# Gated linear attention: queries multiplied at half width and copied into the padded tile by GpSimd; one more block size written by ScalarE

## The chip, the cores and the metric

One core of one Trainium2 chip. Times are microseconds of device time from the start to the end of one execution on that core. A time of a kernel is the median of several executions. The engines are TensorE (PE in the profile), VectorE (DVE), ScalarE (ACT), GpSimd (POOL) and SyncE (SP), which here only issues DMAs.

## The reference

One layer of a decoder trunk, 2048 tokens and 16 learned meta tokens, width 1024, float32. Half of the mixer's heads are gated linear attention (GLA), half attention over a sliding window with a sink; a feed-forward part with a squared ReLU follows.

```
h = h + concat(o_gla, o_swa) @ w_out        # both from rmsnorm(h) @ w_in
h = h + relu(rmsnorm(h) @ w1)^2 @ w2
```

The change is in the GLA half, which the reference writes as a scan over chunks of 64 tokens:

```
b = cumsum(g, axis=2)                                   # log decays, per channel
decay = exp(where(causal, b_i - b_j, -inf))
A = einsum('bhid,bhjd,bhijd->bhij', q, k, decay)
o = einsum('bhij,bhjv->bhiv', A, v) + einsum('bhid,bhdv->bhiv', q * exp(b), S)
S = exp(b_last) * S + einsum('bhjd,bhjv->bhdv', k * exp(b_last - b), v)
```

There are 4 heads of 64 query channels and 128 value channels.

## The kernel before

**The square of scores.** The decay between tokens i and j is a product over the channels, so A is no plain product of q and k. The kernel builds it by levels. `gla_pair` handles 256 tokens (two blocks of 128) at a time, so it runs eight times, as pairs 1 to 8. It holds q and k as `qk` (128 partitions are the channels of two heads; two such head pairs; 256 tokens). For each block size s = 1, 2, 4, 8, 16, 32, 64, `gla_level` multiplies the queries of every odd block of s tokens with the keys of the even block before it (matmuls into the PSUM tile `lv`, L1304), and writes these s x s squares to their places in `AT`, 128 by 128 per head. Then it multiplies the even blocks' keys (L1310) and the odd blocks' queries (L1312) by the level's decay factors from `decays`, so that the next level, with blocks twice as large, finds both relative to the new block borders. Small squares lie on many places of the tile and are written by VectorE through a mask (`copy_predicated`, L1322); for s = 32 and 64 ScalarE copies them (L1315).

**The padded queries.** Two heads share the 128 partitions of a matmul's contraction. To keep them apart, the queries stand in `qpad`, a tile of 128 partitions by 2 heads by 2 head pairs by 256 tokens: head 0 has its values in partitions 0 to 63 and zeros in 64 to 127, head 1 the other way round. The zeros are written once. There is one `qpad` for the whole kernel. At the start of a pair GpSimd copies the queries into it (L1343, L1344), and from then on L1312 multiplies in it, over zeros and values alike: twice as many elements as q has. At the end of a pair `gla_out` multiplies `qpad` with the state S (L1409) and `AT` with v (L1408).

**What runs beside it.** The kernel is mostly dense products in split float32 on TensorE: each weight tile is loaded (`raw`), rounded by ScalarE to a high part (`wh`, L139), and VectorE takes the remainder as the low part (`wl`, L141); three matmuls per tile use them (L178, L179, L180). The tiles `raw`, `wh` and `wl` have three buffers each, and some low parts are stored to DRAM (`lows`) and loaded again later. The GLA pairs run next to the input projection's second half and the feed-forward parts, together with the sliding-window attention: for each block of 128 tokens scores `sc` (L1031, L1032, in two PSUM buffers), a masked copy to `p` with its maximum on VectorE (L1033, with `sst`), exponentials on ScalarE (L1041), the scaling of `p` by GpSimd (L1056), transposes `tr` (L1076) split into `ph` and `pl`, with masks by GpSimd (L1091), the part of the meta tokens (`trm`, `pm` L1065, `ptm` L1068 by GpSimd), `pv`, and outputs `oT` stored to `mix` (by GpSimd's DMA queue at L1114, by SyncE's at L1113).

**What sets the order.** The program is written as Python generators. `drive` (L2230) steps a generator of dense work, and at each of its pauses `mix_stage` (L2237) steps the streams `gla` and `swa` once. The framework then schedules the recorded instructions onto the queues of the engines; on each engine they run in that queue's order, and wait on semaphores for each other. So an edit of one instruction can move others.

Of the kernel before, what the change touches and what calls it, by code (L numbers as in the profile page):

```python
# [13 lines left out]
ALU = mybir.AluOpType  # L14
# [3 lines left out]
P = 128  # L18
# [28 lines left out]
class Layer:  # L47
# [1244 lines left out]
        nc.vector.tensor_copy(eB, factor[P].rearrange("p (a j) -> p a j", a=2))  # L1292
        yield factor, eB

    def gla_level(self, s, qpad, k, AT, factor):

        nc = self.nc
        li = LEVELS.index(s)
        ps = self.gpsum("lv")
        for j in range(2):  # L1300
            for hp in range(2):
                ql = qpad[:, :, hp, j * P : (j + 1) * P].rearrange("p h (n two s) -> p h n two s", two=2, s=s)
                at = (2 * j + hp) * P
                nc.tensor.matmul(  # L1304
                    ps[:, at : at + P], lhsT=k[:, hp, j * P : (j + 1) * P], rhs=ql[:, :, :, 1, :], start=True, stop=True
                )
        n = 256 // s
        f = factor[s].rearrange("p (n two) -> p n two", two=2)
        kv = k.rearrange("p a (n two s) -> p (a n) two s", two=2, s=s)[:, :, 0, :]
        nc.vector.tensor_tensor(kv, kv, f[:, :, 1:2].to_broadcast([P, n, s]), ALU.mult)  # L1310
        qv = qpad.rearrange("p h a (n two s) -> p h (a n) two s", two=2, s=s)[:, :, :, 1, :]
        nc.vector.tensor_tensor(qv, qv, f[:, :, 0:1].unsqueeze(1).to_broadcast([P, 2, n, s]), ALU.mult)  # L1312
        if s >= 32:
            for r in range(0, P, 2 * s):
                nc.scalar.activation(  # L1315
                    AT[r : r + s, :, r + s : r + 2 * s],
                    ps.rearrange("p (h n) -> p h n", h=8)[r : r + s, :, r // 2 : r // 2 + s], AF.Copy,
                )
            return
        av = AT.rearrange("p h (n two s) -> p h n two s", two=2, s=s)  # L1320
        mk = self.lmask[:, li, :].rearrange("p (n s) -> p n s", s=s)
        nc.vector.copy_predicated(  # L1322
            av[:, :, :, 1, :], mk.unsqueeze(1).to_broadcast([P, 8, 64 // s, s]),
            ps.rearrange("p (h n s) -> p h n s", h=8, s=s),
        )

    def gla_pair(self, c, gp, now, outs, state, more):
        nc = self.nc
        qk, gates = now
        qpad, q, k = self.qpad, qk[:, 0:2, :], qk[:, 2:4, :]  # L1330

        next(outs, None)
        yield
        next(outs, None)
        factor, eB = next(gates)
        yield
        next(outs, None)
        next(state, None)
        AT = gp.tile([P, 8, P], F32, name="AT", tag="AT", bufs=1)
        qkp = AT.rearrange("p h n -> p (h n)")[:, :512].rearrange("p (a n) -> p a n", a=2)  # L1340
        nc.vector.tensor_tensor(qkp, q, k, ALU.mult)
        nc.vector.tensor_tensor(q, q, factor[1].rearrange("p (a n) -> p a n", a=2), ALU.mult)
        nc.gpsimd.tensor_copy(qpad[0:64, 0], q[0:64])  # L1343
        nc.gpsimd.tensor_copy(qpad[64:P, 1], q[64:P])  # L1344
        yield
        next(outs, None)
        next(state, None)
        ps = self.pd.tile([P, NB], F32, name="dg", tag="d")
        for j in range(2):
            for hp in range(2):  # L1350
                nc.tensor.matmul(
                    ps[:, 4 * j + 2 * hp : 4 * j + 2 * hp + 2], lhsT=qkp[:, hp, j * P : (j + 1) * P], rhs=self.hsel,
                    start=True, stop=True,
                )
        dg = gp.tile([P, 8], F32, name="dg", tag="dg")
        nc.vector.tensor_copy(dg, ps[:, 0:8])
        for h in range(4):
            nc.scalar.activation(AT[:, h, :], self.ident, AF.Copy, scale=dg[:, h : h + 1])
        yield
        next(outs, None)  # L1360
        for h in range(4, 8):
            nc.scalar.activation(AT[:, h, :], self.ident, AF.Copy, scale=dg[:, h : h + 1])
        v = self.gla_values(c, gp)
        for s in reversed(LEVELS):
            self.gla_level(s, qpad, k, AT, factor)
            yield
            next(outs, None)
            next(state, None)
            if s == LEVELS[1] and more:
                gates = self.gla_front(gp, self.gla_gates(c + 1, gp))  # L1370
                next(gates)
            if s == LEVELS[0]:
                ps = self.pd.tile([P, NB], F32, name="kT", tag="d")
                for j in range(2):
                    for hp in range(2):
                        nc.tensor.transpose(
                            ps[:, (2 * j + hp) * P : (2 * j + hp + 1) * P], k[:, hp, j * P : (j + 1) * P], self.ident
                        )
                kT = gp.tile([P, 4 * P], F32, name="kT", tag="kT")
                nc.scalar.activation(kT, ps, AF.Copy)  # L1380
                if more:
                    next(gates)
                    self.next = self.gla_keys(c + 1, gp), gates
            else:
                yield

        def outs():
            parts = [
                self.gla_out(2 * c + j, gp, AT[:, 4 * j : 4 * j + 4, :], qpad[:, :, :, j * P : (j + 1) * P],
                             kT[:, 256 * j : 256 * j + 256], v[:, j, :], eB[:, :, j : j + 1])  # L1390
                for j in range(2)
            ]
            next(parts[0])
            yield
            yield from parts[0]
            next(parts[1])
            yield
            yield from parts[1]

        return outs()  # L1400
# [1232 lines left out]
```

## Time and profile before

| | |
|---|---|
| median of 3 runs | 2072.09 us (2071.88 to 2073.42) |
| the profiled execution | 2071.57 us, of which its span is 2069.9 |
| mean clock granted to TensorE | 0.998 |
| instructions in the span | 28255 |
| the eight pairs' levels | 243 to 800 us |

How to read the profile's rows: an engine's row gives its busy time, its share of the span and its instructions. A row of a group gives line, engine, operation, output<-inputs, shapes and count, then busy time and mean, then the idle time just before. A row of the timeline gives the start, the duration, the engine, the line and the operation; in brackets stands how long the engine idled before it and what ended that. A row of TensorE's waits gives the matmul that waited, what it waited for, the total, the number and the longest. Ends of matmuls are modelled, and neighbours on an engine overlap a little.

### The profile page before, as it was taken

To read this page: it belongs to the slowest core of one execution; us is meant where nothing else is said; L and a number is where in the kernel's file an instruction comes from. 1 tells how busy PE (TensorE), PEld (TensorE's weight loads), DVE (VectorE), ACT (ScalarE), POOL (GpSimd) and SP (SyncE) were. 2 spreads that over 40 slices of the span, in tenths; PEclk is the share of its full clock that TensorE was granted. 3 is DMA by queue.
4 is the path that set the end of the run, shared out by engine and by line. 5 is a ranking of instruction groups with operands and counts; after the bars stand their busy time and mean duration, and the time that the engine had idled before them with its cause. 6 is when DMAs were issued, how large, how long until landed. Compare 5 with 4: busy or idle time off the path is not lost.

```text
span 2069.9 us, 28255 instructions
## 1 busy us (share of the span) xinstructions
PE 2046.7 (99%) x9995; PEld 1727.0 (83%) x9995; DVE 1572.1 (76%) x2641; ACT 1057.7 (51%) x1975; POOL 223.3 (11%) x378
## 2 busy tenths in 40 slices
PE   9999999999999999999999999999999999999998
PEld 7988799888888888788888888888888888888887
DVE  7867867987998887776666867777766775785876
ACT  7524556565677576554444333443545545333434
POOL 0000134333434332000000000000000000000000
PEclk9999999999999999999999999999999999999999
DMA  7436534556766777935448753496355458654412
GB/s 262 153 121 212 175 90 111 154 151 194 221 188 191 254 241 241 342 108 168 147 143 279 268 191 103 169 326 216 133 177 178 151 180 311 255 191 133 153 50 82
DMA packets 190366, 383.58 MB, mean 185 GB/s; under 512 B 18320, under 2 KB 73872, under 8 KB 190224
## 3 DMA queue, kind: packets, MB, share of 16 engines
q1 hardware_dynamic: 182064, 377.85, 53.8%
q0 software_dynamic: 8160, 3.93, 1.9%
q8 instruction: 78, 1.28, 0.3%
q14 instruction: 64, 0.52, 0.1%
HBM read 260.67 MB, written 120.98 MB: 184 GB/s over the span
## 4 chain that ended last, share of the span: by engine, by line
PE 87%; DVE 7%; DMA 3%; ACT 2%; issue 1%; SPq 0%; POOL 0%; DVEq 0%; ACTq 0%; POOLq 0%
PE psq L179 9%; PE psq L180 9%; PE psq L178 9%; PE psw L179 8%; PE psw L178 8%; PE psw L180 8%; PE psd L179 7%; PE psd L178 7%; PE psd L180 7%; PE psv L653 2%; PE lv L1304 2%; DMA x<-x 1%; PE psd L460 1%; PE psd L461 1%; PE psd L459 1%
## 5 line engine op out<-in xcount | busy, mean ns | idle before, releaser
L180 PE MATMUL psw<-bl,wh 128*128 128x512 f32 x728 | 283.2, 389 | 0.0
L178 PE MATMUL psw<-bh,wh 128*128 128x512 f32 x728 | 283.2, 389 | 0.0
L179 PE MATMUL psw<-bh,wl 128*128 128x512 f32 x728 | 283.2, 389 | 0.0
L178 PE MATMUL psq<-oh,wh 128*128 128x512 f32 x672 | 262.2, 390 | 0.0
L180 PE MATMUL psq<-ol,wh 128*128 128x512 f32 x672 | 261.4, 389 | 0.0
L179 PE MATMUL psq<-oh,wl 128*128 128x512 f32 x672 | 261.4, 389 | 0.0
L1604 ACT ACTIVATE wh<-rw 128x1024 fp32r<-128x1024 f32 x91 | 96.5, 1061 | 276.9 <-PE psw L180 242.1
L1605 DVE TENSOR_TENSOR wl<-rw,wh 128x1024 fp32r<-128x1024 f32 x91 | 111.3, 1223 | 111.0 <-ACT wh L1604 111.0
L178 PEld LDWEIGHTS psw<-bh,wh 128*128 128x128 f32 x728 | 136.6, 188 | 28.6
L180 PEld LDWEIGHTS psw<-bl,wh 128*128 128x128 f32 x728 | 136.6, 188 | 28.5
L179 PEld LDWEIGHTS psw<-bh,wl 128*128 128x128 f32 x728 | 136.6, 188 | 28.0
L178 PEld LDWEIGHTS psq<-oh,wh 128*128 128x128 f32 x672 | 126.1, 188 | 26.8 <-issue 0.5
L179 PEld LDWEIGHTS psq<-oh,wl 128*128 128x128 f32 x672 | 126.1, 188 | 26.6 <-issue 0.5
L180 PEld LDWEIGHTS psq<-ol,wh 128*128 128x128 f32 x672 | 126.1, 188 | 26.1
L178 PE MATMUL psd<-u,wh 128*128 128x512 f32 x320 | 129.6, 406 | 1.8 <-DVE st L279 1.1
L179 PE MATMUL psd<-u,wl 128*128 128x512 f32 x320 | 125.8, 393 | 0.1
L180 PE MATMUL psd<-u,wh 128*128 128x512 f32 x320 | 125.7, 393 | 0.0
L1604 ACT ACTIVATE wh<-r 128x1024 fp32r<-128x1024 f32 x56 | 59.3, 1060 | 114.0 <-PE psq L180 107.0
L2498 DVE TENSOR_TENSOR bl<-b,bh 128x1024 fp32r<-128x1024 f32 x91 | 110.8, 1218 | 0.2
L139 ACT ACTIVATE wh<-raw 128x1024 fp32r<-128x1024 f32 (+2 forms) x70 | 73.0, 1044 | 68.1 <-PE psd L180 46.2
L178 PE MATMUL psd<-m,wh 128*128 128x512 f32 x256 | 101.7, 397 | 0.0
L179 PE MATMUL psd<-m,wl 128*128 128x512 f32 x256 | 100.0, 391 | 0.4 <-DVE wl L1751 0.4
(438 smaller groups left out, 4959.7 us busy)
## 6 DMA issues: line engine op xcount, KB each, us to landing
r<-w SPq DMA_DIRECT2D x56, 512.0 KB
rw<-w2q SPq DMA_DIRECT2D x52, 512.0 KB
b<-hops SPq DMA_DIRECT2D x49, 512.0 KB
b<-hops_j SPq DMA_DIRECT2D x42, 512.0 KB
wl<-lows SPq DMA_DIRECT2D x39, 512.0 KB
raw<-w SPq DMA_DIRECT2D x36, 512.0 KB
raw<-wo SPq DMA_DIRECT2D x32, 512.0 KB
lows<-wl SPq DMA_DIRECT2D x28, 512.0 KB
```

Source lines behind the costliest of these rows:

```text
L139: nc.scalar.activation(wh, raw, AF.Copy)
L178: nc.tensor.matmul(ps, lhsT=wh, rhs=ah, start=first, stop=False, skip_group_check=skip)
L179: nc.tensor.matmul(ps, lhsT=wl, rhs=ah, start=False, stop=False, skip_group_check=skip)
L180: nc.tensor.matmul(ps, lhsT=wh, rhs=al, start=False, stop=last, skip_group_check=skip)
L459: nc.tensor.matmul(ps, lhsT=ah, rhs=wh, start=kt == 0, stop=False)
L460: nc.tensor.matmul(ps, lhsT=ah, rhs=wl, start=False, stop=False)
L461: nc.tensor.matmul(ps, lhsT=al, rhs=wh, start=False, stop=kt == KT - 1)
L653: nc.tensor.matmul(ps, lhsT=x, rhs=y[:, w], start=new and i == 0 and k == 0 and n == 0, stop=i == 1 and k == 1 and n == 2, skip_group_chec ...
L1304: nc.tensor.matmul(ps[:, at : at + P], lhsT=k[:, hp, j * P : (j + 1) * P], rhs=ql[:, :, :, 1, :], start=True, stop=True)
L1604: nc.scalar.activation(wh, src, AF.Copy)
L1605: return (wh, wl), lambda: nc.vector.tensor_tensor(wl, src, wh.bitcast(F32), ALU.subtract)
L2498: self.nc.vector.tensor_tensor(l, self.B[s], h.bitcast(F32), ALU.subtract)
```

## The change

`gla_level` gets `q`, the half of `qk` that holds the queries, beside `qpad`. It multiplies the odd blocks in `q`, 128x256 elements without the zeros, and GpSimd copies the multiplied blocks into `qpad`, with one copy per head on 64 partitions: two copies per level, 112 in all. And the squares of block size 16 go to `AT` by ScalarE, with four copies of 16 partitions, where VectorE's masked copy wrote them; L1322 runs 32 times instead of 40. The copies at a pair's start are now written as a loop and are the same instructions. Behind the edit the lines of the file move by four or five (L1322 is L1326, L1469 is L1474).

```diff
-    def gla_level(self, s, qpad, k, AT, factor):
+    def gla_level(self, s, qpad, q, k, AT, factor):
...
         nc.vector.tensor_tensor(kv, kv, f[:, :, 1:2].to_broadcast([P, n, s]), ALU.mult)
-        qv = qpad.rearrange("p h a (n two s) -> p h (a n) two s", two=2, s=s)[:, :, :, 1, :]
-        nc.vector.tensor_tensor(qv, qv, f[:, :, 0:1].unsqueeze(1).to_broadcast([P, 2, n, s]), ALU.mult)
-        if s >= 32:
+        qv = q.rearrange("p a (n two s) -> p (a n) two s", two=2, s=s)[:, :, 1, :]
+        nc.vector.tensor_tensor(qv, qv, f[:, :, 0:1].to_broadcast([P, n, s]), ALU.mult)
+        for h in range(2):
+            r = slice(64 * h, 64 * h + 64)
+            pv = qpad[r, h].rearrange("p a (n two s) -> p (a n) two s", two=2, s=s)[:, :, 1, :]
+            nc.gpsimd.tensor_copy(pv, qv[r])
+        if s >= 16:
             for r in range(0, P, 2 * s):
                 nc.scalar.activation(
...
-        nc.gpsimd.tensor_copy(qpad[0:64, 0], q[0:64])
-        nc.gpsimd.tensor_copy(qpad[64:P, 1], q[64:P])
+        for h in range(2):
+            r = slice(64 * h, 64 * h + 64)
+            nc.gpsimd.tensor_copy(qpad[r, h], q[r])
...
-            self.gla_level(s, qpad, k, AT, factor)
+            self.gla_level(s, qpad, q, k, AT, factor)
```

The instructions are scheduled anew, and some stand elsewhere. Three places follow, the rows of one engine each: line, operation, output<-inputs, shape, count. The first is GpSimd in pair 8, over the last levels, before:

```order
L1056 TENSOR_SCALAR p<-p,sst 128x128 x4
L1114 DMA mix<-oT 64x4x128
L1056 TENSOR_SCALAR p<-p,sst 128x128 x4
L1068 TENSOR_SCALAR ptm<-pm_1849,vecs 128x128 x4
L1091 AFFINE_SELECT ph<-ph 128x512
L1091 AFFINE_SELECT pl<-pl 128x512
```

And of the change:

```order
L1056 TENSOR_SCALAR p<-p,sst 128x128 x4
L1316 COPY qpad<-qk 64x16x16 x2
L1056 TENSOR_SCALAR p<-p,sst 128x128 x4
L1316 COPY qpad<-qk 64x8x32 x2
L1114 DMA mix<-oT 64x4x128
L1068 TENSOR_SCALAR ptm<-pm_1849,vecs 128x128 x4
L1316 COPY qpad<-qk 64x4x64 x2
L1091 AFFINE_SELECT ph<-ph 128x512
L1091 AFFINE_SELECT pl<-pl 128x512
```

The copies of a level stand behind the attention's steps of four `p` scalings, and ahead of the next such step; the store of `mix` moved behind two of them.

The second place is VectorE in pair 7, around block sizes 4 and 8, with the numbers of the tiles. The three `wl` there are the low parts of three weights that follow each other. Before:

```order
L1312 TENSOR_TENSOR qpad_1851<-qpad_1851,decays_7012 128x128x4
L1322 COPY_PREDICATED AT_7264<-lmask_320,lv_7561 128x128x4
L1469 TENSOR_TENSOR m_7636<-mx_7631,m_7636 128x512
L141 TENSOR_TENSOR wl_7658<-raw_7655,wh_7657 128x1024
L1033 ISA p_7608,sst_7609<-sc_7610,tabs_316 128x272
L1033 ISA sst_7609 128x1
L1033 ISA p_7608,sst_7609<-sc_7614,tabs_316 128x272
L1033 ISA sst_7609 128x1
L141 TENSOR_TENSOR wl_7738<-raw_7735,wh_7737 128x1024
L1065 TENSOR_TENSOR pm4_1849<-trm_7600,pm4_1849 64x128
L1558 TENSOR_TENSOR h_5967<-h_5967,psd_7576 128x512
```

And of the change:

```order
L1326 COPY_PREDICATED AT_7366<-lmask_320,lv_7667 128x128x4
L1312 TENSOR_TENSOR qk_7215<-qk_7215,decays_7112 128x32x8
L141 TENSOR_TENSOR wl_7768<-raw_7765,wh_7767 128x1024
L141 TENSOR_TENSOR wl_7853<-raw_7850,wh_7852 128x1024
L1065 TENSOR_TENSOR pm4_1849<-trm_7708,pm4_1849 64x128
L1033 ISA p_7716,sst_7717<-sc_7718,tabs_316 128x272
L1033 ISA sst_7717 128x1
L1033 ISA p_7716,sst_7717<-sc_7722,tabs_316 128x272
L1033 ISA sst_7717 128x1
L1563 TENSOR_TENSOR h_6043<-h_6043,psd_7684 128x512
```

The two reads of scores (L1033) moved behind the second `wl` and behind `pm`; the multiply of the queries for block size 8 stands ahead of the first `wl`, one level earlier than before.

The third place is VectorE in pair 6, ahead of and around block size 2. Before, the low part `wl_6714` of a weight of `w1` stands among the end of the previous pair's work:

```order
L912 TENSOR_TENSOR kr_1846<-ft_6281,kr_1846 64x128
L1422 TENSOR_TENSOR o_6421<-o_6412,gst_6422 128x512
L1052 TENSOR_TENSOR p_6285<-p_6285,sst_6286 128x64
L141 TENSOR_TENSOR wl_6714<-raw_6711,wh_6713 128x1024
L1432 TENSOR_TENSOR S_1850<-S_1850,kv_6493 64x256
L92 SCALAR_TENSOR_TENSOR nt_6481<-psn_6477,ny_6480 128x512
```

In the change the low part of the same weight is `wl_6803`:

```order
L1310 TENSOR_TENSOR qk_6341<-qk_6341,decays_6238 128x128x2
L1326 COPY_PREDICATED AT_6520<-lmask_320,lv_6738 128x256x2
L920 TENSOR_TENSOR vc_6784<-vr_6368,vc_6784 128x2x64
L920 TENSOR_TENSOR vd_6788<-vr_5974,vd_6788 128x2x64
L141 TENSOR_TENSOR wl_6803<-raw_6800,wh_6802 128x1024
L1538 SCALAR_TENSOR_TENSOR fr_6760<-psd_6725,rb_6564 128x512
L1312 TENSOR_TENSOR qk_6341<-qk_6341,decays_6238 128x64x4
L141 TENSOR_TENSOR wl_6880<-raw_6877,wh_6879 128x1024
```

It moved by some 30 rows, to behind the masked copy of block size 2 and the two steps `vc` and `vd` that prepare values for the attention. TensorE's products with it, `psd`, stand where they stood, and so does nearly every other matmul.

## The prediction

> **What bounds the kernel now.** I read the page's busy times and its chain first, then the table of windows, then TensorE's waits.
>
> ```profile
> PE 2046.7 (99%) x9995; PEld 1727.0 (83%) x9995; DVE 1572.1 (76%) x2641; ACT 1057.7 (51%) x1975; POOL 223.3 (11%) x378
> ...
> PE 87%; DVE 7%; DMA 3%; ACT 2%; issue 1%; SPq 0%; POOL 0%; DVEq 0%; ACTq 0%; POOLq 0%
> ```
>
> TensorE is busy 99% of the span and holds 87% of the chain that ended last. An edit to VectorE, ScalarE and GpSimd can pay only through TensorE's idle time. Where is that, in the stretch that the change touches? The edited levels run from 243 to 800 us; the next rows are two of eight windows, one per pair of chunks, the sum of the eight, and a window behind the levels (from:to, length, then busy time with its count per engine, granted clock, DMA share, GB/s).
>
> ```profile
> 311.00:380.00 69.00, 66.09 (x440) 62.08 (x439) 55.73 (x149) 44.09 (x128) 28.22 (x46) 1.00 0.50 140
> ...
> 673.00:747.00 74.00, 71.52 (x394) 61.08 (x393) 62.77 (x159) 48.51 (x131) 27.24 (x46) 1.00 0.81 260
> ...
> sum 550.00, PE 542.91 PEld 473.60 DVE 464.09 ACT 351.68 POOL 210.66; mean PE 67.86 PEld 59.20 DVE 58.01 ACT 43.96 POOL 26.33
> ...
> 900.00:1000.00 100.00, 100.00 (x441) 82.45 (x440) 72.09 (x96) 50.80 (x73) 0.00 (x0) 1.00 0.44 146
> ```
>
> In those 550 us TensorE idles 550.00 - 542.91 = 7.1 us; from 900 us on there is nothing left to win. VectorE idles 86 us there, so it is loaded but not full. What ended the long waits of TensorE (total, times, longest):
>
> ```profile
> PE psd L459 <- ACT st L466: 2.0, 1, 2.0
> PE psd L179 <- DVE wl L141: 1.4, 1, 1.4
> PE sc L1031 <- DVE sst L1033: 1.3, 2, 1.1
> ...
> PE tr L1076 <- POOL p L1056: 0.6, 1, 0.6
> ```
>
> The 2.0 us on ScalarE lie in the second pair (317.6 us). So VectorE and GpSimd cause at most 7.1 - 2.0 = **5.1 us**, the most the change can win. No row has TensorE waiting for `qpad` or `lv`: what the change speeds up is never waited for now.
>
> **The change, part by part.** Per-line durations (min/median/max in ns):
>
> ```profile
> L1310 DVE TENSOR_TENSOR qk<-qk,decays x56: 392/424/858, 245.3 to 794.8; 128x256 f32<-128x256 f32 x56
> L1312 DVE TENSOR_TENSOR qpad<-qpad,decays x56: 676/684/1130, 245.6 to 795.6; 128x512 f32<-128x512 f32 x56
> L1322 DVE COPY_PREDICATED AT<-lmask,lv x40: 686/720/1330, 246.2 to 781.9; 128x512 f32<-128x512 uint8 x40
> L1315 ACT ACTIVATE AT<-lv 32x256 f32<-32x256 f32 x16 | 5.9, 368 | 0.5 <-PE lv L1304 0.4
> L1343 POOL COPY qpad<-qk x8: 602/604/1505, 221.9 to 741.4; 64x512 f32<-64x512 f32 x8
> L1056 POOL TENSOR_SCALAR p<-p,sst x128: 361/370/1961, 241.4 to 790.6; 128x128 f32<-128x128 f32 x128
> ```
>
> *VectorE.* 56 multiplies of 128x512 become 56 of 128x256, the shape of L1310: 56 x (684 - 424) = 14.6 us less. Eight copies of L1322 go, at 0.72 each 5.8 us. That is 20 us less in 464, on an engine that is off the chain for most of this stretch. Alone it is worth only what it takes from the 5.1 us.
>
> *ScalarE.* Block size 16 needs four activations per pair, 32 in all. They are smaller (16 partitions by 128 elements) than the 32x256 row at 0.368; I take 0.31 to 0.37, 10 to 12 us more. ScalarE has 198 of the 550 us free. Its result `AT` is first read at the pair's end, so I cost it at nothing; if ScalarE were late by a whole group of four, 1.5 us of casts behind it would be late, still ahead of most readers.
>
> *GpSimd.* 112 copies of 64x256 are new, and no row has this shape. A line through 128 elements at 0.361 and 512 at 0.602 gives about 0.44 (an estimate from rows of two operations), so 0.9 us for the two of a level and 49 us in all. Bounds: 0.36 each (the 128-element row) and 1.5 each (the longest 512-element copy, made beside VectorE work): 0.7 to 3.0 us per pair. The likeliest is 0.9, since both rows are mostly at their minimum. GpSimd goes from 211 to 260 of 550 us.
>
> *The new wait.* The next level's `lv` product used to wait for a VectorE multiply; now it also waits for two GpSimd copies, which stand in GpSimd's queue behind softmax scaling (`p`, `ptm`), masks and `mix` stores. Behind the copies, in turn, wait those operations and TensorE's transposes of `p`. For each of the 48 gaps between two levels of a pair I took the end of the GpSimd work ahead of the copies plus 0.9 us against the start of the next `lv`. Most leave 2 to 6 us. Six leave under 1 us; the tightest and one more:
>
> ```profile
> 424.84 2.70 POOL L1056 TENSOR_SCALAR p<-p,sst 128x128 f32<-128x128 f32 x4
> 428.26 1.05 PE L1304 MATMUL lv<-qpad,qk 128*128 128x128 f32 x8
> ...
> 789.46 2.31 POOL L1056 TENSOR_SCALAR p<-p,sst 128x128 f32<-128x128 f32 x4
> ...
> 793.17 1.05 PE L1304 MATMUL lv<-qpad,qk 128*128 128x128 f32 x8
> ```
>
> At 424.84 + 2.70 + 0.9 = 428.44 the copies are done, 0.2 after the product's start; at 789.46 + 2.31 + 0.9 = 792.67 they are 0.5 before it. The other four leave 0.4, 0.6, 0.9 and 1.0. With the estimate the six cost 0.2 us, with half a microsecond of stretch at each 0.8; the work ahead of the copies may stretch too, so **+1.0** (0 to +2.5).
>
> *Order, pair 7 (the first moved place).* The reads of the first score pair (L1033) stood between two low-part products `wl`; now they stand behind both and behind `pm`.
>
> ```profile
> 697.88 0.43 DVE L1033 CUSTOM_DVE_ANT_0 p<-sc,tabs 128x272 f32<-128x272 f32 x1
> ...
> 699.26 1.23 DVE L141 TENSOR_TENSOR wl<-raw,wh 128x1024 fp32r<-128x1024 f32 x1 [0.59 <-ACT wh L139]
> 700.52 0.29 DVE L1065 TENSOR_TENSOR pm<-trm,pm 64x128 fp32r<-64x128 f32 x1
> ...
> 698.52 0.37 PE L1031 MATMUL sc<-kr,qs 128*128 128x272 f32 x1
> ...
> 703.51 0.39 PE L1031 MATMUL sc<-kr,qs 128*128 128x272 f32 x1 [1.06 <-DVE sst L1033]
> ```
>
> The second `wl` waits for ScalarE's `wh`, hence for a weight's DMA, and can't come earlier. So the first read starts at 700.52 + 0.29 = 700.8 and ends at 701.2. The next scores, due at 698.52, need its PSUM buffer (there are two): a new wait of 2.7. In return the third pair's reads are earlier against TensorE, and the 1.06 at 703.51 goes: **+1.6** (0 to +2.7; 0 if the pair's earlier relief lets the weight's DMA start sooner).
>
> *Order, pair 6 (the second).* A `w1` weight's low part, made at 595.52, now stands behind `vd`. TensorE's products with it begin at 612.94.
>
> ```profile
> 595.52 1.23 DVE L141 TENSOR_TENSOR wl<-raw,wh 128x1024 fp32r<-128x1024 f32 x1
> ...
> 614.26 0.72 DVE L920 TENSOR_TENSOR vd<-vr,vd 128x128 fp32r<-128x128 f32 x1
> 614.90 1.65 DVE L141 TENSOR_TENSOR wl<-raw,wh 128x1024 fp32r<-128x1024 f32 x1
> ...
> 612.51 0.67 PE L1076 MATMUL tr<-tabs,p 128*128 128x128 f32 x2 [0.56 <-POOL p L1056]
> 612.94 0.48 PE L178 MATMUL psd<-f,wh 128*128 128x512 f32 x1
> 613.26 0.40 PE L179 MATMUL psd<-f,wl 128*128 128x512 f32 x1
> ```
>
> With no relief it would start at 614.90 and end at 616.1, 2.9 after 613.26. Ahead of it VectorE loses that product itself (1.2), the difference of two q multiplies (0.5) and a residual step that moved behind it (0.7); some of this is lost again where the queue waits for ScalarE's exponentials. I take 1.7 of relief, a wait of 1.2, under which the 0.56 of `p` may also vanish: **+1.0** (-0.6 to +2.9).
>
> *What goes.* The q multiply of a level now stands one level earlier on VectorE, so at a pair's start two short ones take the place of one long one and nothing is gained; from block size 8 on the queue runs 0.3 to 1 us ahead. Of the 5.1 us, 1.06 is used above, and the 1.4 hangs on a weight's arrival. I credit half of the remaining 2.6: **-1.3** (0 to -4).
>
> **Sum:** 1.0 + 1.6 + 1.0 - 1.3 = +2.3. The profiled execution took 2071.57 (span 2069.9), half a microsecond under the median of 2072.09 and just under the fastest shown, 2071.88; +2.3 on the median is **2074.4**.
>
> **GpSimd beside VectorE.** Four `p` steps took:
>
> ```profile
> 449.30 1.41 POOL L1056 TENSOR_SCALAR p<-p,sst 128x128 f32<-128x128 f32 x4
> ...
> 484.52 3.57 POOL L1056 TENSOR_SCALAR p<-p,sst 128x128 f32<-128x128 f32 x4 [1.22 <-DVE vc L920]
> ```
>
> The second stood beside a row of VectorE multiplies and took 2.5 times as long. The Trainium skill, SBUF — State Buffer, section "Who interferes with whom", says that a VectorE instruction with two SBUF inputs and a GpSimd instruction that reads SBUF exclude each other for whole instructions. That speaks against this change, which adds 112 such reads, and these two rows agree with it. By it at its worst each copy holds up a multiply for its whole length, 49 us on VectorE against the 20 gained, and the time would be that of rival 1 below, 2083.6; by the medians of the rows it is the forecast's.
>
> **Rivals.**
> 1. *The copies are slow* (ends slower). If copies meet VectorE multiplies as at 484.52, and take up to the longest L1343 row, a level's two cost 3.0 instead of 0.9. The 2.1 more eat the six tight gaps (9.4 us in sum: six times 2.1 less the 3.2 that they leave) and two more gaps of 1.7 and 1.8 (0.7): 10.2 in place of the 1.0. 2072.1 + 10.2 + 1.3 = 2083.6. It passes 4.1 us from about 1.9 us per level on. For it: row 484.52. Against it: the medians lie at the minimum. The page named above points to this rival.
> 2. *VectorE's relief wins* (faster). The moved reads and the moved weight cost nothing because the queue runs ahead, and all 5.1 go: 2067.0. Against it: the 1.4 and the second `wl` of pair 7 hang on DMAs, not on VectorE.
> 3. *It makes no difference*: the copies fit in every gap, the moved rows find cover: 2072.1, give or take 1. For it: no wait on `lv` today, 2 to 6 us in most gaps.
> 4. *The moved weight is late in full*, and the buffer that it frees late delays a later weight's load: +2.9 at once and up to 3 more: 2078 to 2080.
>
> **How the numbers follow.** My forecast (2072.5 to 2076.2) gets 0.50, no difference 0.17, slow copies 0.13, late weight 0.12, relief 0.08. About 0.2% (4.1 us) is what a measurement can tell from no change. Faster, below 2067.9: 0.05, most of the relief rival. Slower, above 2076.2: slow copies and late weight 0.25, and 0.03 for the forecast's bounds: 0.28. The rest, 0.67, lies within. For 8 in 10 the range runs from 2068.5, just short of the full relief, to 2081, where the slow copies are already at some 2.5 us per level; its lower part serves the bound of -4 of the credit.
>
> **What would show it.** Right: VectorE about 20 us lower in the windows, GpSimd about 49 higher, L1316 at 0.4 to 0.6 us, TensorE waits for `qpad` in one to four places of under 1 us, a wait for `sst` near 698, one for `wl` near 613. Wrong: L1316 above 0.9 in the median (rival 1), TensorE idle in the levels under 4 us (rival 2), or above 14 us, which would mean a wait that I don't see.

## The result, and the profile after

The changed kernel takes 2089.67 us in the median of five runs (2088.63 to 2091.42), the kernel before 2073.42 in the five runs beside it (2071.88 to 2073.88). The ratio is 1.0080 with a 95% interval of 1.0069 to 1.0091: the change costs 16 us. The forecast was 2074.4 with a range up to 2081; its centre lay on the slower side, but at a seventh of the size, and the measured time lies outside the range. The profiled execution of the change took 2091.12, its span 2089.4; the profiled execution before lies under its median and this one above, so the two spans are 19.5 us apart.

The page's busy times after:

```profile
PE 2054.7 (98%) x9995; PEld 1730.7 (83%) x9995; DVE 1554.0 (74%) x2633; ACT 1064.5 (51%) x2007; POOL 279.6 (13%) x490
```

VectorE has 18 us less to do, as computed (20), ScalarE 7 more (10 to 12), GpSimd 56 more (49). The work is where it was expected. But TensorE idles 15.5 us between 243 and 800 us (557.00 less 541.53 busy), against 7.1 before; the prediction named more than 14 as the sign of a wait that it didn't see. What ended TensorE's long waits (total, times, longest):

```profile
PE psd L178 <- DVE pm L1065: 6.0, 2, 3.0
PE psd L178 <- ACT wh L139: 2.6, 1, 2.6
PE psd L179 <- DVE wl L141: 2.6, 2, 1.3
PE psd L178 <- DVE st L279: 2.1, 2, 1.6
PE psd L459 <- ACT st L466: 2.0, 1, 2.0
PE lv L1304 <- POOL qpad L1316: 1.8, 2, 1.1
```

The first row has grown most: 6.0 us behind `pm`, a small VectorE step of the attention, against this row before:

```profile
PE psd L178 <- DVE pm L1065: 0.5, 1, 0.5
```

The wait that the prediction named, `lv` behind GpSimd's copies, is 1.8 us. So VectorE does less and yet is late. Why? Its groups show it, and GpSimd's (busy, mean ns | idle time before, and what ended it). The first row is the query multiply before, the others are the change's:

```profile
L1312 DVE TENSOR_TENSOR qpad<-qpad,decays 128x512 f32<-128x512 f32 x56 | 42.5, 759 | 0.0
...
L1310 DVE TENSOR_TENSOR qk<-qk,decays 128x256 f32<-128x256 f32 x56 | 25.9, 462 | 20.0 <-PE lv L1304 19.9
L1312 DVE TENSOR_TENSOR qk<-qk,decays 128x256 f32<-128x256 f32 x56 | 25.3, 451 | 29.0 <-POOL qpad L1316 26.2 <-POOL qpad L1349 2.3
...
L1316 POOL COPY qpad<-qk 64x256 f32<-64x256 f32 x112 | 65.4, 584 | 49.3 <-PE lv L1304 44.0 <-DVE pl L1080 2.0
```

VectorE idles 26.2 us, in 21 places, before the query multiply, ended by GpSimd's copies; before, it didn't idle there (0.0). The multiply of a level writes into blocks of `q` that the copies of the level before still read, so it must wait for them. The copies in turn wait for `lv` (44.0 us), since they overwrite the padded tile that `lv` reads.

One place in full, pair 4, in the timeline of VectorE, GpSimd and TensorE (start, duration, engine, line; in brackets the idle time before and what ended it):

```profile
499.82 0.41 DVE L1310 TENSOR_TENSOR qk<-qk,decays 128x256 f32<-128x256 f32 x1
502.34 0.42 DVE L1312 TENSOR_TENSOR qk<-qk,decays 128x256 f32<-128x256 f32 x1 [2.10 <-POOL qpad L1316]
502.68 0.68 DVE L1080 TENSOR_TENSOR pl<-tr,ph 128x512 fp32r<-128x512 f32 x1
503.40 0.28 DVE L1065 TENSOR_TENSOR pm<-trm,pm 64x128 fp32r<-64x128 f32 x1
...
497.38 4.14 POOL L1056 TENSOR_SCALAR p<-p,sst 128x128 f32<-128x128 f32 x4 [4.68 <-DVE vd L920]
501.47 0.84 POOL L1316 COPY qpad<-qk 64x256 f32<-64x256 f32 x2
...
500.31 0.38 PE L1145 MATMUL lr<-tabs,lr 128*16 128x128 f32 x2
503.74 0.79 PE L178 MATMUL psd<-u,wh 128*128 128x512 f32 x1 [3.05 <-DVE pm L1065]
```

GpSimd scales `p` beside a row of VectorE multiplies and takes 4.14 us for it. The copies start behind it at 501.47. VectorE has finished the key multiply at 500.23 and stands before the query multiply until 502.34. Behind that stand `pl` and `pm`; `pm` frees a PSUM buffer (L1062) that the next weight's products need; so TensorE idles 3.05 us. The copies were not needed before the next `lv`, several microseconds later.

Then a second cost. The windows after this wait (window, length, busy times, granted clock, DMA share, GB/s):

```profile
501.70:503.70 2.00, 0.00 (x0) 0.00 (x0) 1.31 (x3) 0.13 (x1) 1.55 (x3) 1.00 0.76 255
503.70:505.70 2.00, 1.96 (x5) 1.58 (x6) 1.96 (x3) 0.00 (x0) 1.84 (x3) 0.50 0.98 164
505.70:507.70 2.00, 2.00 (x8) 1.57 (x6) 0.40 (x1) 0.37 (x1) 0.53 (x2) 0.65 0.80 312
507.70:509.70 2.00, 2.00 (x15) 1.78 (x14) 0.42 (x1) 0.44 (x1) 0.41 (x1) 1.00 0.81 205
```

After the wait TensorE is granted 0.50 and 0.65 of its clock in these two windows: 2 x 0.50 + 2 x 0.35 = 1.7 us more are lost. It happens three times in the change (at the waits that end at 503.7, 657.9 and 861.1 us) and not once between 200 and 2060 us before; over windows of 4 us, the missing share of the clock sums to 5.2 us. TensorE's waits from 200 to 900 us sum to 23.6 us in the timeline, against 13.0 before. So 10.6 us of waits and 5.2 of clock make 15.8 of the 19.5 us between the two spans. Of the rest, some 1.6 us are in the clock between 50 and 70 us, ahead of the changed levels (0.83 in the mean, 0.91 before), and 0.8 is a wait at 1415.8 us; 1.3 is not accounted for. Not all of the 5.2 belongs to the copies: the wait at 861.1 (2.63 us, for a weight's high part `wh`) stands in the kernel before too, as 2.44 at 843.9, but there the clock stayed full.

### The profile page after: what moved, and what is told of

The parts are those of the page before. It is cut to its first block, busy times and chain, and to the rows that moved or that the text cites. A ratio compares the mean times of both kernels' runs of the same rounds, so it can differ in the third digit from the quotient of the medians.

```text
span 2089.4 us, 28482 instructions
## 1 busy us (share of the span) xinstructions
PE 2054.7 (98%) x9995; PEld 1730.7 (83%) x9995; DVE 1554.0 (74%) x2633; ACT 1064.5 (51%) x2007; POOL 279.6 (13%) x490
## 4 chain that ended last, share of the span: by engine, by line
PE 58%; DVE 1%; DMA 1%; ACT 0%; issue 0%; SPq 0%; DVEq 0%; ACTq 0%
PE psq L178 9%; PE psq L179 9%; PE psq L180 8%; PE psw L178 8%; PE psw L180 8%; PE psw L179 8%; PE psd L180 3%; PE psd L179 3%; PE psd L178 3%; DMA raw<-w 1%; DMA raw<-wo 0%; DVE hu L1648 0%; PE psn L108 0%; ACT wh L139 0%; DVE acc L1598 0%
```

## Experiments

Each is timed in five rounds beside the kernel before, whose median was 2073.1 to 2073.4 us in these sessions; ratios are to it, with their 95% intervals. **The theory**: the loss comes from VectorE's query multiply waiting, at the head of its queue, for GpSimd's copies. **The rivals**: the block size moved to ScalarE; the rows that the scheduler moved (order); the copies' load on GpSimd and their contention with VectorE.

**1. Block size 16 alone.** In the kernel before:

```diff
-        if s >= 32:
+        if s >= 16:
```

> The kernel before with one part of the change: block size 16 is written to the square by ScalarE; queries are multiplied in the padded tile as before, and nothing is copied within the levels. Theory (the wait): the loss of 16 us comes from VectorE's query multiply, which must wait until GpSimd has copied the queries of the level before, and holds VectorE's queue meanwhile; here that wait can't be, so 2070 to 2075 us against 2073 before, and TensorE idles 7 to 9 us from 243 to 800 us. Rival 'block 16': the four small ScalarE copies are to blame: 2080 to 2090.

2074.69 us, ratio 1.0007 (0.9998 to 1.0015), and TensorE idles 7.8 us from 243 to 800 us. This part costs nothing that can be told apart from no change.

**2. The queries alone.** In the change:

```diff
-        if s >= 16:
+        if s >= 32:
```

> The change without its second part: block size 16 stays with VectorE's masked copy; queries are multiplied at half width and copied by GpSimd. Theory (the wait): the loss stays, 2084 to 2094 us; VectorE idles 20 to 30 us before the query multiply, ended by GpSimd's copies. Rival 'block 16': back to 2070 to 2076.

2083.02 us, ratio 1.0047 (1.0035 to 1.0059): most of the loss, though 1 us under the expected range. VectorE idles 25.2 us for the copies. TensorE's waits from 200 to 900 us sum to 19.2 us, and the clock loses 1.7. The two parts don't add up (1.6 + 9.9 against 16). In the traces the difference stands in good part at the second wait on `pm` (1.4 us here, 2.9 with the change) and in the clock (1.7 against 5.2). The first wait on `pm` is as long here (3.00 us at 502.2), but the clock stays full behind it (the last section shows why the two differ); why ScalarE's part makes the second wait longer was not tried. The profiled execution here was also the fastest of its five, 2.9 us under their median.

**3. The multiply put behind the key multiply.** The whole change, and:

```diff
-        nc.vector.tensor_tensor(kv, kv, ...)
+        km = nc.vector.tensor_tensor(kv, kv, ...)
...
-        nc.vector.tensor_tensor(qv, qv, ...)
+        with self.tc.issue_after(km.ins):
+            nc.vector.tensor_tensor(qv, qv, ...)
```

> The whole change, with one edit: a level's query multiply is queued on VectorE behind the same level's key multiply. The key multiply waits for the level's lv product, and that product has already waited for the copies of the level before, so the query multiply finds them done. The same instructions run, GpSimd has the same 112 copies. Theory (the wait): VectorE's idle time before the query multiply that copies end falls from 26 us to under 4, and the time to 2070 to 2078. Rival 'contention' (copies beside VectorE's multiplies stretch both): 2084 to 2092 as with the change, since the copies are all there. Rival 'order' (moved rows around the scores and a weight): 2080 to 2090, as long as those rows stand where the change put them.

2074.25 us, ratio 1.0002 (0.9993 to 1.0011): the loss is gone, with all 112 copies in place. The groups of this kernel:

```profile
L1313 DVE TENSOR_TENSOR qk<-qk,decays 128x256 f32<-128x256 f32 x56 | 27.6, 493 | 0.0
...
L1317 POOL COPY qpad<-qk 64x256 f32<-64x256 f32 x112 | 62.2, 555 | 74.6 <-DVE qk L1313 55.0 <-PE trm L1063 7.3 <-PE tr L1076 6.4
```

The 29.0 us are 0.0. Contention is refuted as the cause: the same copies are made here and take about as long (555 ns in the mean against 584). But the edit also puts VectorE's other rows back nearly where they stood before the change, so it doesn't tell the wait from the order. Experiment 5 does.

**4. No copies.** The change without its copies:

```diff
-            nc.gpsimd.tensor_copy(pv, qv[r])
```

> The change without GpSimd's 112 copies: the padded tile keeps the pair's first queries, so the scores of block sizes above 1 and the term with the state are computed from queries without the levels' decays. All other instructions stay. What does the half-width multiply gain by itself? Theory (the wait): neither the wait nor the load of GpSimd is there: 2066 to 2073. Rival 'order': 2078 to 2090.

2085.21 us, ratio 1.0059 (1.0047 to 1.0071). A miss: neither wait nor copies, and yet 12 us slower. The timeline at the first pair:

```profile
221.75 0.89 DVE L1312 TENSOR_TENSOR qk<-qk,decays 128x256 f32<-128x256 f32 x2 [1.36 <-POOL qpad L1345]
...
222.75 2.25 DVE L1312 TENSOR_TENSOR qk<-qk,decays 128x256 f32<-128x256 f32 x5
```

With nothing that holds them to their levels, all seven multiplies of a pair are ready at its start, and the scheduler issues them there: 3.1 us of VectorE in one piece. TensorE then waits 2.7 us at 228.8 us for a VectorE step on a product (`st`). The clock loses 10.2 us after such waits. Experiment 6 has the same instructions with the multiplies kept at their levels, and takes 2074.50. So order can cost nearly as much as the wait; this experiment says nothing on the change, whose order is another.

**5. The order of the change without its wait.** The copies read the keys' odd blocks, which no VectorE instruction of the next level overwrites ahead of `lv`, and the query multiply is pinned where the change has it:

```diff
+        ko = k.rearrange("p a (n two s) -> p (a n) two s", two=2, s=s)[:, :, 1, :]
...
-            nc.gpsimd.tensor_copy(pv, qv[r])
+            nc.gpsimd.tensor_copy(pv, ko[r])
...
-        nc.vector.tensor_tensor(qv, qv, ...)
+        with self.tc.issue_after(self.km.ins) if s > 1 else contextlib.nullcontext():
+            nc.vector.tensor_tensor(qv, qv, ...)
+        self.km = km
```

> The change with its order kept and its wait taken away. GpSimd's 112 copies read the same number of elements from the keys' odd blocks in place of the queries' (so the scores are computed from the wrong values), and each query multiply is pinned on VectorE behind the key multiply of the level before, where the change has it. TensorE's and ScalarE's rows then stand exactly as in the change, VectorE's and GpSimd's but for a few neighbours. Nothing holds VectorE's query multiply to GpSimd any more. Theory (the wait): 2073 to 2079 us, VectorE's idle time before the query multiply under 3 us (the pair's first copies aside), and no wait of TensorE above 2 us on pm. Rival 'order': 2083 to 2090, since all rows stand as in the change; experiment 3 would then have worked by putting the rows back. Rival 'contention': 2083 to 2090 too, with VectorE's multiplies and GpSimd's scalings as stretched as in the change.

2074.59 us, ratio 1.0010 (1.0001 to 1.0018). The same place in pair 4:

```profile
495.66 0.51 DVE L1310 TENSOR_TENSOR qk<-qk,decays 128x256 f32<-128x256 f32 x1
496.09 0.41 DVE L1313 TENSOR_TENSOR qk<-qk,decays 128x256 f32<-128x256 f32 x1
496.43 0.68 DVE L1080 TENSOR_TENSOR pl<-tr,ph 128x512 fp32r<-128x512 f32 x1
497.14 0.28 DVE L1065 TENSOR_TENSOR pm<-trm,pm 64x128 fp32r<-64x128 f32 x1
...
492.93 3.73 POOL L1056 TENSOR_SCALAR p<-p,sst 128x128 f32<-128x128 f32 x4 [4.16 <-DVE vd L920]
496.61 0.84 POOL L1319 COPY qpad<-qk 64x256 f32<-64x256 f32 x2
```

The rows are those of the change, in the same order (over the whole kernel TensorE's and ScalarE's all are, VectorE's and GpSimd's but for five). `p` is nearly as stretched (3.73 us), and the copies come nearly as late behind it; but the query multiply follows the key multiply at once, `pm` starts before the copies are done, and TensorE has no wait there. VectorE's idle time before the query multiply is that behind the pair's first copies alone:

```profile
L1313 DVE TENSOR_TENSOR qk<-qk,decays 128x256 f32<-128x256 f32 x56 | 27.1, 484 | 2.4 <-POOL qpad L1352 2.3
```

This decides for the wait, against order and contention: 15 of the 16 us go with it. The rest, 1.2 us or 0.1%, is at the edge of what can be told apart.

**6. What can half-width multiplies win?** Experiment 3 without the copies:

```diff
-            nc.gpsimd.tensor_copy(pv, qv[r])
```

> Experiment 3 (query multiply behind the key multiply) without the 112 copies: the padded tile keeps the pair's first queries, so later scores lack the levels' decays. What is the most that 20 us less of VectorE can win, with neither copies nor wait, and VectorE's queue in the order of before? My estimate from TensorE's 7 us of idle time in the levels: 2068 to 2073 us. Rival 'contention': experiment 3 is held back by the copies, and this one is faster than it by 4 us or more. Theory (the wait): it is within 3 us of experiment 3.

2074.50 us, ratio 1.0004 (0.9995 to 1.0013). With VectorE relieved of 20 us, with no copies and no wait, nothing is won that can be told apart; my estimate of up to 5 us was too high. It equals experiment 3, so copies that hardly anything waits for cost nothing to speak of either.

**7. The copies on ScalarE**, on top of experiment 3:

```diff
-            nc.gpsimd.tensor_copy(pv, qv[r])
+            nc.scalar.activation(pv, qv[r], AF.Copy)
```

> Experiment 3 with the 112 copies on ScalarE in place of GpSimd. Could the idea win with another engine? ScalarE gets about 35 to 40 us more in 550 and has 170 free. GpSimd's queue no longer stands between levels, so lv has no wait for GpSimd; but the copies must wait for lv at the head of ScalarE's queue, ahead of exponentials and of weights' high parts. I expect 2073 to 2082; below 2069 it would beat the kernel before.

2076.60 us, ratio 1.0016 (1.0006 to 1.0026): no better than on GpSimd. The copies' wait for the multiply, at the head of ScalarE's queue, is now 38.7 us in 24 places.

**8. The change with every copy made twice**, and **9. experiment 3 with every copy made twice**:

```diff
-            nc.gpsimd.tensor_copy(pv, qv[r])
+            for _ in range(2):
+                nc.gpsimd.tensor_copy(pv, qv[r])
```

> The change with every copy of the levels made twice (224 copies, the same result). A larger dose: a level's copies take 1.7 us instead of 0.84. Theory (the wait): VectorE's idle time before the query multiply, 26 us with the change, grows by 0.84 us in each of the 21 places that wait and in some more, to 42 to 60 us, and the time by 8 to 25 us over the change, to 2098 to 2115. Rival 'only GpSimd's load on the lv gaps': as with the next kernel, 4 to 7 us.

2106.34 us, ratio 1.0162 (1.0148 to 1.0176), 17 us more than the change. VectorE's group there:

```profile
L1312 DVE TENSOR_TENSOR qk<-qk,decays 128x256 f32<-128x256 f32 x56 | 23.9, 426 | 59.8 <-POOL qpad L1317 57.5 <-POOL qpad L1350 2.3
```

The wait grows from 26.2 to 57.5 us, and the loss doubles with it.

> Experiment 3 (query multiply behind the key multiply) with every copy made twice. VectorE's queue doesn't wait for copies here; only the next lv does. Theory (the wait): the six tight gaps between levels lose 0.84 us more each, 4 to 7 us over experiment 3's 2074: 2077 to 2082; TensorE's waits for the padded tile grow from 1.7 to 5 to 9 us. Rival 'contention': GpSimd's 47 us more stretch VectorE as a whole, 2085 or more.

2084.98 us, ratio 1.0057 (1.0045 to 1.0070), 10.7 us above experiment 3 where 4 to 7 were expected. TensorE's waits there:

```profile
PE lv L1304 <- POOL qpad L1318: 7.9, 7, 3.0
```

They grew from 1.7 to 7.9 us, within 5 to 9 as expected. What was not priced is the clock after them: 6.8 us are missing between 200 and 2060 us, against 3.4 in experiment 3. The time is at the edge of what the rival gave (2085 or more), so it alone doesn't refute contention, and VectorE's busy time is 5.6 us above that of experiment 3 (1559.1 against 1553.5). But contention isn't needed to explain the time: 6.2 us of waits and 3.4 of clock make 9.6 of the 10.7.

None of these kernels is faster than the kernel before; the best, experiment 3, equals it.

## Why the prediction failed

**What bounds the kernel, and the cap on the gain: right.** With a cap of 5.1 us little could come of it, and experiment 6, the change's gain without its costs, shows none.

**The durations: right.** The half-width multiply has a median of 425 ns (424 taken). The new copies have a median of 415 and a mean of 584 ns (estimate 440, bounds 360 to 1500), so the pair takes 0.84 us in the place shown, against 0.9. VectorE loses 18 us (20).

**The new wait: the step that failed.** The prediction named one new wait, that of `lv` on the copies, and followed the queue behind the copies on GpSimd. It priced that wait at 1.0 us; it measured 1.8, at 550.6 and 582.8 us, not at the two gaps shown. But the copies also read `q`, and the next level's multiply writes `q`. That second wait stands on VectorE, and the part "What goes" booked its row, the multiply one level earlier in the queue, as relief. It was the reverse: the multiply stood where the copies that it depends on were not yet done, and 21 times VectorE's whole queue stood with it. Experiment 5 takes just this wait away and finds 15 of the 16 us; experiment 3 takes it away together with the order and finds as much. So the credit of -1.3 was the term with the wrong sign, and the sum had no term at all for the wait that made nearly the whole loss. That the forecast's centre lay on the slower side was luck: it came from the moved rows and from `lv`, and not from this wait. Both facts were on the table: the diff shows `qv[r]` read by GpSimd, and the rows of order show the next `qk` multiply right behind the masked copy. A row moved ahead should have been asked which other engine must be done first.

**Moved weight in pair 6: right.** A wait of 1.2 us for `wl` was computed, with a relief that was a choice; 1.22 came at 624.7 us, and again 1.22 in experiment 5, which keeps that order. That it agrees to the hundredth is chance. The 0.56 on `p` went, as allowed for.

**Moved scores in pair 7: mechanism right, size wrong.** The score product waits for L1033 behind the second `wl` and `pm`, as said, but 1.11 us instead of 2.7, and the 1.06 of the next pair goes: net 0, not +1.6. The second weight's high part began 5.3 us after its DMA was issued (711.95 - 706.67), against 6.7 before (698.17 - 691.46), so the whole chain was earlier. The bound of zero, "if the pair's earlier relief lets the weight's DMA start sooner", was right in size; but the DMA was issued at the same time relative to TensorE, and it was its flight that was shorter.

**The rivals.** Slow copies gave 2083.6 by way of `lv`; the copies were not slow in the median, and `lv` hardly waited. What was slow was GpSimd's scaling of `p` ahead of them: at 497.38 four scalings took 4.14 us beside VectorE's multiplies, and the copies came late behind it, but VectorE's own sum fell as computed. The Trainium skill's rule on VectorE and GpSimd reads (SBUF — State Buffer, "Who interferes with whom") agrees with the stretch on GpSimd's side; no run here isolates it, and no cost on VectorE's side shows. The late weight cost 1.2 us and not 2.9 and more, and the full relief did not come.

**The clock was missing from every price.** A wait of 2 to 3 us was counted at its length, though many cost up to 1.7 us more.

## What to carry to other kernels

When an operation is split and one half goes to another engine, list both new waits: who needs the result, and who next overwrites what the other engine reads. Then ask what stands behind that second waiter in its own queue: an engine can have less work and be later. If the overwriting step is not needed early, queue it behind something that has already waited for the other engine; here that cost one line and won back the whole loss, but this kernel, in which TensorE is busy 99% of the time, gains nothing from VectorE's relief either way.

## What the runs showed of the hardware that had not been expected

- **Waits of about 2 us slow TensorE's clock, if they fall into one stretch of a grid.** In these traces the granted clock falls to a half for 3.41 us at a time (1.7 us lost) at waits of 1.8 to 3.1 us (1.81 at 708.1 us in experiment 4, 2.04 at 851.4 in experiment 2, 3.05 here at 503.7). Not every such wait does it: 2.44 us before at 843.9, 3.00 in experiment 2 at 502.2 and 2.98 in experiment 5 at 845.7 did not. The traces tell them apart. The falls within a trace stand whole multiples of 3.41 us from each other (here the second 153.6 us and the third 358.4 us behind the first: 45 and 105 of them). On a grid of 3.41 us laid through them, the wait of 3.05 us fell into one stretch, with 2.99 us of idle time in it. The 3.00 was split over two, with 1.24 and 1.76, the 2.98 with 1.81 and 1.17, the 2.44 with 1.06 and 1.38. From 60 to 2050 us of all eleven traces, 21 stretches at full clock hold at least 1.85 us of idle time, and each was followed by half clock; of those with less, two were (1.81 and 1.48). So a wait of 2 to 3 us can cost 1.7 us more or nothing more, by where it falls, and the clock's part in a difference between two traces is partly chance. The Trainium skill (TensorE: Matmul & The Clock Gate, "Part 1: The HAM clock gate (the "warmup" mystery)") gives a free-running window of about 3.4 us; the traces agree with its length.
- **GpSimd's scaling of four tiles took 4.14 us beside VectorE's two-input multiplies**, and 1.41 at 449.3 us before; the new copies ranged from 0.386 to 1.412 us each for the same shape.
